# Row sums of 64 MiB: each partition takes 128 consecutive rows instead of eight groups of 16

## Chip, cores, metric

One core of one Trainium2 chip. The metric is the device time of one execution in microseconds (us).

## The reference

```python
batch, seq, dim = 32, 512, 1024
x = np.random.randn(batch, seq, dim).astype(np.float32)   # 67.1 MB
def reference(x):
    return np.sum(x, axis=-1).astype(np.float32)          # 16,384 sums
```

Every input byte is read once and added once; the output is 64 KB.

## The kernel before

The 16,384 rows are split over 128 partitions, 128 rows each. VectorE and ScalarE, two of the core's engines, sum rows out of on-chip tiles. The SP queue issues the loads, and 16 DMA engines carry them out in packets, here one packet for each contiguous run of a partition (896 of 64 KiB for the seven large loads). The rows are divided by groups: group g is a solid block of 2,048 rows (8 MiB), in which partition p has the 16 rows from 16p. Partitions that follow one another are therefore 64 KiB apart in device memory. The last group is split: its first 7 rows are the first load of the kernel, its last 9 rows the last four loads.

```python
    BIG, FIRST, pieces = 16, 7, (560, 464)
    x_g = x.flatten_outer_dims().rearrange("(g p j) d -> g p j d", p=P, j=BIG)
    out_v = out.rearrange("b s -> (b s)").rearrange("(g p j) -> p g j", p=P, j=BIG)
    def rows_from(j, n):
        return x_g[j // BIG, :, j % BIG : j % BIG + n, :]
    last = J // BIG - 1
    # ... three input buffers; rows() = one load and the sums of its rows
    t = inpool.tile([P, BIG * dim + 4], fp32)
    rows(t, 0, FIRST, last * BIG, 0)                    # 7 rows of the last group
    for g in range(last):                               # seven loads of 16 rows, 8 MiB each
        t = inpool.tile([P, BIG * dim + 4], fp32)
        if g < last - 1:
            load = rows(t, 0, BIG, g * BIG, 0)          # one VectorE reduce of 16 rows
        else:
            rows(t, 0, BIG, g * BIG, 7, pairs=True)     # 9 rows VectorE, 7 ScalarE
    # ... 6 rows, 2 rows, the last row in pieces of 560 and 464 elements
    hold(store(nc.scalar, 0, last), two, "its packets come behind those of the loads")
    # ... the last sums
    store(nc.sync, last, last + 1)
```

## Time and profile before

| | before |
|---|---|
| time, median of 3 runs | 161.56 us |
| span of the profiled execution | 160.0 us |
| first load landed | 11.10 us |
| last load landed | 157.90 us |
| load queue, share of the 16 DMA engines | 97.7% |
| VectorE busy | 120.6 us (75%) |
| one 16-row reduce, and the distance between two | 17.22 us, 19.36 us |

The DMA engines set the pace, since a tile takes 19.36 us to load and 17.22 us to sum. The lines that carry this are in the prediction.

### The profile page before, as it was taken

The page shows a single profiled execution, that of the slowest core. Times are in us where ns is not written, and L with a number is a line of the kernel's source. Part 1 is how long each engine was busy: PE and PEld are TensorE (multiplying, and loading weights), DVE is VectorE, ACT ScalarE, POOL GpSimd, SP SyncE. Part 2 cuts the span into 40 slices and gives each one's busy share as a digit, 9 for nine tenths or more (in the row PEclk, how much of TensorE's full clock was granted, in tenths as well). Part 3 has the DMA queues.
Part 4 walks back from the last instruction along what each step waited for, and adds up shares of the span by engine and source line. Part 5 has one row for each costly group of instructions (what it writes and reads, how often), then busy time and mean ns, then how long its engine had stood idle before and what let it go on. Part 6 is the DMA issues. An engine that isn't in the chain of part 4 may idle for free.

```text
span 160.0 us, 134 instructions
## 1 busy us (share of the span) xinstructions
DVE 120.6 (75%) x40; ACT 11.9 (7%) x21; POOL 0.2 (0%) x4
## 2 busy tenths in 40 slices
DVE  0029600399995999779995899949999499994955
ACT  3000000000000000000000000000000000003993
POOL 0000000000000000000000000000000000000000
DMA  8899899799699699699699798996996996996994
GB/s 322 365 491 524 377 410 524 328 459 524 278 508 524 262 524 524 262 524 524 262 524 442 344 524 377 410 524 262 524 524 262 524 524 262 524 524 264 424 384 123
DMA packets 2784, 67.18 MB, mean 420 GB/s; under 512 B 1248, under 2 KB 1376, under 8 KB 1504
## 3 DMA queue, kind: packets, MB, share of 16 engines
q1 hardware_dynamic: 1872, 67.12, 97.7%
q10 hardware_dynamic: 912, 0.06, 0.4%
HBM read 67.11 MB, written 0.07 MB: 420 GB/s over the span
## 4 chain that ended last, share of the span: by engine, by line
DMA 71%; DVE 27%; SPq 1%; issue 0%; DVEq 0%
DMA t<-in_x_dram 71%; DVE sums L167 26%; SPq L206 0%; SPq L248 0%; DVE t L181 0%; DVEq L279 0%
## 5 line engine op out<-in xcount | busy, mean ns | idle before, releaser
L167 DVE TENSOR_REDUCE sums<-t 128x16 f32<-128x16384 f32 (+1 forms) x7 | 110.9, 15848 | 33.7 <-DMA t<-in_x_dram 33.7
L194 ACT ACTIVATE unread<-t 128x1024 f32<-128x1024 f32 x10 | 10.1, 1013 | 145.1 <-DMA t<-in_x_dram 145.1
L181 DVE CUSTOM_DVE_ANT_0 t<-t 128x512 f32<-128x512 f32 (+2 forms) x16 | 9.6, 657 | 4.0 <-DMA t<-in_x_dram 3.8
L194 ACT ACTIVATION_READ_ACCUMULATOR unread<-t 128x1 f32 x10 | 1.9, 187 | 0.0
L194 ACT ACT_TABLE_LOAD x1 | 1.3, 1283 | 0.8 <-PEq L268 0.8
L181 DVE DVE_READ_ACCUMULATOR2_ANT sums<- 128x1 f32 x15 | 1.3, 84 | 0.0
L268 POOL MEMSET const-bfloat16-1.0<- 128x1 bf16 x1 | 0.1, 101 | 0.0
L268 POOL MEMSET const-uint8-127<- 128x1 uint8 x1 | 0.1, 101 | 0.0
L268 POOL MEMSET const-float32-0.0<- 128x1 f32 x1 | 0.1, 98 | 0.2 <-issue 0.2
L268 POOL MEMSET const-float32-1.0<- 128x1 f32 x1 | 0.1, 98 | 0.0
L181 DVE DVE_READ_ACCUMULATOR2_ANT t<- 128x1 f32 x1 | 0.1, 83 | 0.0
L246 DVE MEMSET t<- 128x1 f32 x1 | 0.1, 59 | 0.0
## 6 DMA issues: line engine op xcount, KB each, us to landing
t<-in_x_dram SPq DMA_DIRECT2D x1, 3584.0 KB, 11.1
t<-in_x_dram SPq DMA_DIRECT2D x1, 3072.0 KB, 28.8
t<-in_x_dram SPq DMA_DIRECT2D x1, 1024.0 KB, 30.9
t<-in_x_dram SPq DMA_DIRECT2D x1, 280.0 KB, 31.2
t<-in_x_dram SPq DMA_DIRECT2D x1, 232.0 KB, 31.2
t<-in_x_dram SPq DMA_DIRECT2D x7, 40.9
out_dram<-sums ACTq DMA_DIRECT2D x1, 56.0 KB, 2.1
out_dram<-sums SPq DMA_DIRECT2D x1, 8.0 KB, 1.4
```

What stands on the lines that cost most here:

```text
L167: return nc.vector.tensor_reduce(out=dst, in_=src, axis=mybir.AxisListType.X, op=mybir.AluOpType.add)
L181: return nc.vector.tensor_tensor_reduce(out=src[:, :n], in0=src[:, :n], in1=src[:, n:], scale=1.0, scalar=0.0, op0=mybir.AluOpType.add, op ...
L194: nc.scalar.activation(out=unread[:, :n], in_=src, func=mybir.ActivationFunctionType.Copy, accum_out=dst,)
L246: nc.vector.memset(whole[:, width + 1 :], 0.0)
L268: nc = _bacc.Bacc("TRN2", target_bir_lowering=False, num_devices=1)
```

## The change

Each partition now owns 128 consecutive rows. The stated arrangement of loads (7 rows, seven times 16, then 6, 2 and the last row in two pieces) stays. The code becomes simpler, the early store is one run of 448 bytes per partition instead of seven of 64, and in every load the partitions lie 512 KiB apart instead of 64 KiB. This distance is called the pitch below. Lines left out of the cut also make each tile 16 bytes shorter and put the last nine rows at the start of their tile.

```diff
-    x_g = x.flatten_outer_dims().rearrange("(g p j) d -> g p j d", p=P, j=BIG)
-    out_v = out.rearrange("b s -> (b s)").rearrange("(g p j) -> p g j", p=P, j=BIG)
-    def rows_from(j, n):
-        return x_g[j // BIG, :, j % BIG : j % BIG + n, :]
+    x_p = x.flatten_outer_dims().rearrange("(p j) d -> p j d", p=P)
+    out_p = out.rearrange("b s -> (b s)").rearrange("(p j) -> p j", p=P)
 ...
-            load = nc.sync.dma_start(out=block, in_=rows_from(j, n))
+            load = nc.sync.dma_start(out=block, in_=x_p[:, j : j + n, :])
 ...
-        rows(t, 0, FIRST, j, 0)
+        rows(t, 0, FIRST, 0, 0)
 ...
-                load = rows(t, 0, BIG, g * BIG, 0)
+                load = rows(t, 0, BIG, FIRST + g * BIG, 0)
 ...
-        hold(store(nc.scalar, 0, last), two, "its packets come behind those of the loads")
+        done = J - BIG
+        stored = nc.scalar.dma_start(out=out_p[:, :done], in_=sums[:, :done])
+        hold(stored, two, "its packets come behind those of the loads")
 ...
-        store(nc.sync, last, last + 1)
+        nc.sync.dma_start(out=out_p[:, done:], in_=sums[:, done:])
```

More of the change, by code (lines that the diff above doesn't have):

```diff
@@ L143 @@
     BIG = 16
-    x_g = x.flatten_outer_dims().rearrange("(g p j) d -> g p j d", p=P, j=BIG)
-    out_v = out.rearrange("b s -> (b s)").rearrange("(g p j) -> p g j", p=P, j=BIG)
-    def rows_from(j, n):
-        return x_g[j // BIG, :, j % BIG : j % BIG + n, :]
-    last = J // BIG - 1
+    x_p = x.flatten_outer_dims().rearrange("(p j) d -> p j d", p=P)
+    out_p = out.rearrange("b s -> (b s)").rearrange("(p j) -> p j", p=P)
     FIRST = 7
+    full = J // BIG - 1
     pieces = (560, 464)
@@ L214, in rows @@
             return load
-        def store(eng, g0, g1):
-            return eng.dma_start(
-                out=out_v[:, g0:g1],
-                in_=sums[:, g0 * BIG : g1 * BIG].rearrange("p (g j) -> p g j", j=BIG),
-            )
-        j = last * BIG
-        t = inpool.tile([P, BIG * dim + 4], fp32)
-        rows(t, 0, FIRST, j, 0)
+        t = inpool.tile([P, BIG * dim], fp32)
+        rows(t, 0, FIRST, 0, 0)
         first = sums_of[-1]
-        for g in range(last):
-            t = inpool.tile([P, BIG * dim + 4], fp32)
-            if g < last - 1:
-                load = rows(t, 0, BIG, g * BIG, 0)
+        for g in range(full):
+            t = inpool.tile([P, BIG * dim], fp32)
+            if g < full - 1:
+                load = rows(t, 0, BIG, FIRST + g * BIG, 0)
@@ L231 @@
             else:
-                rows(t, 0, BIG, g * BIG, 7, pairs=True)
+                rows(t, 0, BIG, FIRST + g * BIG, 7, pairs=True)
             if g == 1:
                 hold(load, first, "no descriptors of later loads while the first ones start")
-        t = inpool.tile([P, BIG * dim + 4], fp32)
-        rows(t, FIRST, 6, j + FIRST, 2, pairs=True)
-        two = rows(t, FIRST + 6, 2, j + FIRST + 6, 1, pairs=True)
-        a = BIG - 1
-        j += a
+        t = inpool.tile([P, BIG * dim], fp32)
@@ L244 @@
+        rows(t, 0, 6, J - 9, 2, pairs=True)
+        two = rows(t, 6, 2, J - 3, 1, pairs=True)
         c, width = pieces
-        whole = t[:, a * dim + c : BIG * dim + 2]
+        part = t[:, 8 * dim : 8 * dim + c]
+        whole = t[:, 8 * dim + c : 9 * dim + 2]
         nc.vector.memset(whole[:, width + 1 :], 0.0)
-        part = t[:, a * dim : a * dim + c]
-        nc.sync.dma_start(out=part, in_=rows_from(j, 1)[:, 0, :c])
-        nc.sync.dma_start(out=whole[:, 1 : width + 1], in_=rows_from(j, 1)[:, 0, c:])
@@ L250 @@
-        hold(store(nc.scalar, 0, last), two, "its packets come behind those of the loads")
+        nc.sync.dma_start(out=part, in_=x_p[:, J - 1, :c])
+        nc.sync.dma_start(out=whole[:, 1 : width + 1], in_=x_p[:, J - 1, c:])
+        done = J - BIG
+        stored = nc.scalar.dma_start(out=out_p[:, :done], in_=sums[:, :done])
+        hold(stored, two, "its packets come behind those of the loads")
         halves(whole[:, :1], part)
-        halves(sums[:, j : j + 1], whole)
-        store(nc.sync, last, last + 1)
+        halves(sums[:, J - 1 : J], whole)
```

## The prediction

> **What bounds the kernel now.** The whole input, 67.1 MB, must come in once, so I read the page for DMA first: the share of the queues, then the fill of the slices.
>
> ```profile
> DMA  8899899799699699699699798996996996996994
> GB/s 322 365 491 524 377 410 524 328 459 524 278 508 524 262 524 524 262 524 524 262 524 442 344 524 377 410 524 262 524 524 262 524 524 262 524 524 264 424 384 123
> ...
> q1 hardware_dynamic: 1872, 67.12, 97.7%
> q10 hardware_dynamic: 912, 0.06, 0.4%
> HBM read 67.11 MB, written 0.07 MB: 420 GB/s over the span
> ```
>
> The load queue keeps the 16 engines busy 97.7% of the span. The swing from 262 to 524 is only counting: a packet's bytes are booked where it ends, and packets are as long as a slice or so. Longer windows smooth it.
>
> ```profile
> 12.00:31.00 19.00, 7.30 (x2) 0.00 (x0) 0.00 (x0) 1.00 1.02 442
> 31.00:50.00 19.00, 16.87 (x2) 0.00 (x0) 0.00 (x0) 1.00 1.02 442
> 50.00:69.00 19.00, 17.02 (x1) 0.00 (x0) 0.00 (x0) 1.00 1.02 442
> 69.00:88.00 19.00, 17.22 (x1) 0.00 (x0) 0.00 (x0) 1.00 0.99 424
> ```
>
> Columns: window, its length, VectorE, ScalarE and GpSimd busy, clock, DMA share, GB/s. In each window the engines are full and VectorE is not. The timeline says the same by its idle times.
>
> ```profile
> 49.80 17.22 DVE L167 TENSOR_REDUCE sums<-t 128x16 f32<-128x16384 f32 x1 [2.13 <-DMA t<-in_x_dram]
> 69.16 17.22 DVE L167 TENSOR_REDUCE sums<-t 128x16 f32<-128x16384 f32 x1 [2.14 <-DMA t<-in_x_dram]
> 88.65 17.22 DVE L167 TENSOR_REDUCE sums<-t 128x16 f32<-128x16384 f32 x1 [2.27 <-DMA t<-in_x_dram]
> ```
>
> One 16-row tile is 128 x 64 KiB = 8.389 MB. Tiles become ready 19.36 us apart (69.16 - 49.80), a rate of 8.389 MB / 19.36 us = 433 GB/s, and VectorE needs 17.22 us of each interval; it waits 2.13 to 2.27 us every time. So the path is: first load, 56 packets of 64 KiB per DMA engine, the last small loads, the tail. The packet records in the trace make it sharper: 896 packets of 65,536 bytes with a median of 2,418 ns, and three quarters of them under 2,421 ns. 65,536 / 2,418 = 27.1 GB/s per engine, 433.7 GB/s for 16. So even a spread says that they run at one fixed rate[...].
>
> The chain of waits must be read with this in mind:
>
> ```profile
> 67.05 40.99 DMA t<-in_x_dram
> 108.04 0.02 issue
> 108.07 17.23 DVE sums L167
> ...
> 126.68 31.22 DMA t<-in_x_dram
> 157.90 0.06 issue
> 157.96 0.40 DVE t L181
> ```
>
> It puts 26.3% on VectorE, because a load is issued when a reduce frees its buffer (108.07 to 125.30). That is the order of issue, not a bottleneck: the loads issued at 125 us wait behind two others already queued, and land about 31 us later. The last load lands at 157.90, and 2.1 us of tail follow to the end of the span at 160.0. The measured time is 161.56, so 1.5 us lie outside the span.
>
> [...]
>
> [...]
>
> **The change part by part.**
>
> 1. Order of instructions: nothing moves. On VectorE one reduce of 7 rows, six of 16 rows, the same 14 halves of 512, memset and two last pieces; on ScalarE the same ten activations and one store; on the SP queue the same 12 loads with the same bytes per partition and one store. VectorE's 120.6 us and ScalarE's 11.9 us stay: 0. The three buffers rotate over the same nine tiles with the same waits: 0. The tile is 16 bytes shorter: no instruction sees it, 0.
>
> 2. Addresses of the loads. Before, in one load partition p starts at p x 64 KiB, so the 8 MB are one solid block. After, partition p starts at p x 512 KiB (128 rows x 4 KiB), and the block per partition stays 64 KiB solid. Packets keep their size and count: 896 of 64 KiB, 128 each of 28, 24 and 8 KiB, and the two pieces. Only the pitch changes, 64 KiB to 512 KiB, a power of two in both. What it costs is the one real unknown. Worth: bytes / rate = 67.11 MB / 433.7 GB/s = 154.7 us stand on the path, so each 1% of rate is 1.55 us, and it is not hidden: VectorE has 2.1 us per tile of slack in the wrong direction, it only waits longer. [...]here there are only reads[...]. I expect no loss or a small one to be likelier than the whole[...].
>
> 3. The early store (112 of 128 sums per partition). Before, seven runs of 64 B per partition, 896 packets; after, one run of 448 B, 128 packets. Its packets are short: 56 per engine at 8 to 11 ns plus 1 completion, about 0.6 us of engine time, saved to about 0.1 or 0.2. But when does it run? It is issued at 156.69 and lands 2.1 us later; in the records its packets start about 0.2 us after the last load packet has ended, and its last one ends about 0.9 us before the final store's first. It touches neither. So it comes off the busy time of the queue and not off the end: 0, at most -0.1.
>
> 4. Which sums the early store waits for. The new rows 0 to 111 end inside the last 16-row tile, at its nine VectorE rows; ScalarE's seven rows go with the final store. The store was held back by the 2-row load anyway and sits behind ScalarE's activations in its own queue. 0.
>
> 5. The final store. Before: 128 runs of 64 B that form a solid 8 KB; after: 128 runs of 64 B, 512 B apart. Issue to landing was 1.4 us, nearly all of it latency. I expect 1.3 to 1.6: 0.0, plus or minus 0.1 on the path.
>
> Sum: 161.56 + 0 + 1.0 + 0 + 0 + 0 = about 162.5.
>
> **Rivals.**
>
> A. The pitch costs nothing. For: the packets run at a fixed 27.1 GB/s per engine[...], the 64 KiB pitch was itself a large power of two[...]. Then the time is 161.3 to 161.8. This is the likeliest single outcome, about 55%.
>
> B. [...] For: [...]the 16 engines start within 0.8 us of each other. Already before, some tiles show stragglers: in the fourth large load packets of up to 2,528 ns, where the mean went to 2,443 (1% over the median)[...]. [...]
>
> C. The store pays off. For: 768 fewer packets, whole runs of 448 B. Against: step 3, neither lies on the path. At most 161.3. Even with a tail wholly free of store cost, only 2.1 us (1.3%) stand after the last load, so 2% cannot come from there[...]. Faster by 2% needs 158.3 us, which would be 154.7 us of data plus 1.4 us before the first packet plus the 1.5 outside with nearly no tail. I rule it out but for accident.
>
> D. VectorE becomes the bound. Against: its work is the same, 17.22 of 19.36 us per tile, and if loads slow down it gets further from it.
>
> **Range and chances.** Faster cases are bounded by A and C near 161.2. [...] With some 55% at A, 13% in between and 30% over 164.8 (2% over), I give 162.5 us, 161.2 to 167.5.
>
> **What would show it.** If A holds: tiles ready 19.3 to 19.5 us apart, waits of 2.1 to 2.3 us before each 16-row reduce, the 64 KiB packets at a median of 2,418 ns, the last load landing at 157.9. If B: [...]packet times longer and more spread, [...]the whole delay growing in proportion over the seven large loads, not in the tail. Steps 3 to 5: the ACT queue's packets fall from 912 to 144, its landing from 2.1 us to less, while the time from the last load to the end stays about 2.1 us. A change of more than 0.3 us in the tail, a change in VectorE's 17.22 us, or a load issued later relative to its reduce would prove the working wrong; so would a time under 161.

Passages of the prediction that no trace or run of this case shows are cut, at the marks. Its sum came to 162.5 us: the 161.56 us of the kernel before and 1.0 us for step 2. That 1.0 us stands as a bare estimate. Cut too are the sizes and some of the grounds of rival B, which holds that the loads' rate falls with the pitch, and with them what the upper end of the range and the 30% above 164.8 us rested on.

## The result

| | before | after |
|---|---|---|
| median of 6 runs | 161.78 us | 161.94 us |
| lowest to highest | 161.44 to 162.12 | 161.87 to 162.33 |

The ratio is 1.0016, with a 95% interval of 0.9999 to 1.0033. (A ratio is the mean time of one kernel's fast runs over that of the other's of the same rounds, so it is not quite the ratio of the medians.) The change is not clear of noise. The predicted 162.5 us was 0.6% above the 161.56 us that the prediction started from.

The page of the changed kernel, DMA queues:

```profile
q1 hardware_dynamic: 1872, 67.12, 97.4%
q10 hardware_dynamic: 144, 0.06, 0.1%
HBM read 67.11 MB, written 0.07 MB: 419 GB/s over the span
```

The load queue is as full as it was (97.4% against 97.7%). The ScalarE queue's packets fell from 912 to 144 as foreseen, and its store landed in 1.6 us instead of 2.1. The timeline of the changed kernel, with start, duration and, in brackets, the idle time before:

```profile
30.85 17.22 DVE L164 TENSOR_REDUCE sums<-t 128x16 f32<-128x16384 f32 x1 [11.71 <-DMA t<-in_x_dram]
50.20 17.22 DVE L164 TENSOR_REDUCE sums<-t 128x16 f32<-128x16384 f32 x1 [2.13 <-DMA t<-in_x_dram]
...
127.60 17.22 DVE L164 TENSOR_REDUCE sums<-t 128x16 f32<-128x16384 f32 x1 [2.12 <-DMA t<-in_x_dram]
```

Compare the idle times: 2.12 to 2.14 us in every interval, where a stream slower by 1% would have shown 2.3. The first and last of these starts are 96.75 us apart for five tiles, 19.35 us each. The kernel before, over the same five intervals:

```profile
30.45 17.22 DVE L167 TENSOR_REDUCE sums<-t 128x16 f32<-128x16384 f32 x1 [11.70 <-DMA t<-in_x_dram]
...
127.45 17.22 DVE L167 TENSOR_REDUCE sums<-t 128x16 f32<-128x16384 f32 x1 [2.16 <-DMA t<-in_x_dram]
```

That is 97.00 us, so in this pair of profiles the changed kernel's stream is the quicker one, by 0.25 us. The packet records agree: the 896 packets of 64 KiB have a median of 2,418 ns in both, and a mean of 2,426.5 ns before and 2,420.3 ns after. What went the other way is the start. The chain of waits of the changed kernel:

```profile
0.00 11.50 DMA t<-in_x_dram
...
126.85 31.18 DMA t<-in_x_dram
158.03 0.04 issue
158.07 0.40 DVE t L178
```

The first load lands at 11.50 us (before: 11.10), the last at 158.03 (before: 157.90). So in these two profiles 0.40 us are lost at the start and 0.27 come back in the stream. Two questions follow: is the lost start real, and does the stream, at 2,418 ns per packet with both pitches, escape because it is made of loads or because its runs are long?

### The profile page after: what moved, and what is told of

It is laid out like the page before. It is cut to its first block, busy times and chain, and to the rows that moved or that the text cites. A ratio compares the mean times of both kernels' runs of the same rounds, so it can differ in the third digit from the quotient of the medians.

```text
span 160.1 us, 134 instructions
## 1 busy us (share of the span) xinstructions
DVE 120.6 (75%) x40; ACT 11.9 (7%) x21; POOL 0.2 (0%) x4
## 3 DMA queue, kind: packets, MB, share of 16 engines
q1 hardware_dynamic: 1872, 67.12, 97.4%
## 4 chain that ended last, share of the span: by engine, by line
DMA 71%; DVE 27%; SPq 1%; issue 0%; DVEq 0%
DMA t<-in_x_dram 71%; DVE sums L164 26%; SPq L203 0%; SPq L235 0%; DVE t L178 0%; DVEq L268 0%
```

## The experiments

Kernels called wrong on purpose read or write permuted rows, so that one address pattern can be changed alone; their instructions, bytes and waits are those of the kernel that they start from.

### Which part of the change: loads and stores crossed

`a1_after_again` is the changed kernel again. `a2_newloads_oldstores` gives it the output addresses of before, `a3_oldloads_newstores` the reverse.

```diff
 a2, in the changed kernel
-    out=out_p[:, :done], in_=sums[:, :done]                # the final store likewise
+    out=out_g[:, :7], in_=sums[:, :done].rearrange("p (g j) -> p g j", j=BIG)
 a3, in the kernel before
-    out=out_v[:, g0:g1], in_=sums[:, g0 * BIG : g1 * BIG].rearrange(...)
+    out=out_p[:, g0 * BIG : g1 * BIG], in_=sums[:, g0 * BIG : g1 * BIG]
```

> The changed kernel once more, with five rounds. Theory 1 (the pitch costs the steady stream nothing[...]): 64 KiB packets at a median of 2,418 to 2,420 ns, ratio to before 1.000 to 1.003. Theory 2 (a small cost of the pitch at the start of a stream, seen as the first load landing at 11.5 instead of 11.1 us): the first load lands at 11.4 us or later in this profile again and the ratio is 1.001 to 1.003. Theory 3 (the 0.16% is spread of the runs): the first landing is anywhere between 11.0 and 11.6 us and the interval holds 1.

> Loads of the changed kernel (pitch 512 KiB), stores with the addresses of the kernel before (runs of 64 B, so the sums land in wrong places: the result is wrong on purpose). If the stores are off the path: same time as the changed kernel within 0.2 us, 912 packets on the ScalarE queue, its store landing after 2.1 us. If the shorter early store had gained something that the pitch took away: 0.3 us or more above the changed kernel, ratio to before 1.003 to 1.005.

> Loads of the kernel before (pitch 64 KiB), stores with the addresses of the changed kernel (448 B runs and 64 B at 512 B; the result is wrong on purpose). If the stores are off the path: ratio to before 0.999 to 1.001, the early store lands after 1.6 us, the final one after 1.4 us. If the new stores gain on the path: ratio 0.998 or less. If the first landing of 11.1 belongs to the 64 KiB pitch, it is below 11.3 us here; if it is chance, it may be anything from 11.0 to 11.6.

| five rounds, same chip | loads | stores | median us | ratio to before, 95% | first load landed |
|---|---|---|---|---|---|
| before | 64 KiB | 64 B runs | 161.51 | | |
| a1 | 512 KiB | 448 B runs | 162.01 | 1.0022 (1.0002 to 1.0041) | 11.52 |
| a2 | 512 KiB | 64 B runs | 161.87 | 1.0021 (1.0001 to 1.0041) | 11.33 |
| a3 | 64 KiB | 448 B runs | 161.47 | 0.9990 (0.9974 to 1.0006) | 10.98 |

With the new loads the ratio is 1.002 whichever the stores, and the interval just excludes 1; with the old loads it is 1 within the interval. So the stores are off the path within this noise, and the first landing goes with the loads. One line of a1's timeline shows that the steady stream repeats what the first profile of the change showed:

```profile
108.27 17.22 DVE L164 TENSOR_REDUCE sums<-t 128x16 f32<-128x16384 f32 x1 [2.13 <-DMA t<-in_x_dram]
```

### The disputed cost by itself: copies and loads at four pitches

The prediction argued for a cost of the pitch from copies within the device memory; no run had shown it. So copies are measured here beside loads. Four kernels first copy all rows into scratch memory (32 copies of 128 x 16 KiB), copy that a second time into another scratch array, and then run the changed kernel on the second copy. Source and target of the second copy have the same pitch: a solid block (b1), 512 KiB, 516 KiB or 2 MiB. The cut is of the last three; b1 copies 512 rows at a time as solid blocks, and its final loads have a pitch of 512 KiB.

```diff
+        far = far_t.rearrange("(p j) d -> p j d", p=P)      # far_t: [P * rows, dim] in device memory,
+        far2 = far2_t.rearrange("(p j) d -> p j d", p=P)    # rows = 128, 129 or 512 per partition
+        for i in range(0, J, 4):
+            nc.sync.dma_start(out=far[:, i : i + 4, :], in_=x_p[:, i : i + 4, :])
+        for i in range(0, J, 4):
+            nc.sync.dma_start(out=far2[:, i : i + 4, :], in_=far[:, i : i + 4, :])
+        x_p = far2
```

> All rows are copied twice within the device memory (32 copies of 128 x 16 KiB, each a solid 2 MB block on both sides), then the loads of the changed kernel read the second copy at a pitch of 512 KiB. The pass of interest is the second copy, memory to memory, and the final loads. Theory 1[...]: the second copy takes 2 x 67.1 MB / 433 GB/s = 310 us if both directions share one limit, or 155 us if read and write of one packet overlap; the final loads have 64 KiB packets at 2,418 ns as from the input.

> The same, every pass at a pitch of 512 KiB on both sides. [...] Final loads: 2,418 ns per 64 KiB packet under theory 1; 2,500 ns if pure reads suffer from the pitch at all.

> The same with a pitch of 516 KiB (129 rows) in the scratch memory, no power of two. [...] Final loads at 2,418 ns per 64 KiB packet.

> The same with a pitch of 2 MiB in the scratch memory. [...] The final loads tell two theories apart. Theory 1a (loads [...]only lose beyond some pitch): they slow visibly here, 64 KiB packets at 2,600 ns or more. Theory 1b ([...]the loss belongs to copies, where the writes have the pitch too): 2,418 to 2,440 ns here as well.

All four gave correct results. Time in windows (window, length, VectorE, ScalarE and GpSimd busy, clock, DMA share, GB/s, each packet counted once): the first line is inside the first copy, the second inside the second, the third inside the final loads. First 516 KiB, no power of two:

```profile
5.00:200.00 195.00, 0.00 (x0) 0.00 (x0) 0.00 (x0) 1.00 1.00 317
220.00:410.00 190.00, 0.00 (x0) 0.00 (x0) 0.00 (x0) 1.00 1.00 321
455.00:550.00 95.00, 84.33 (x6) 0.00 (x0) 0.00 (x0) 1.00 1.00 433
```

Then 512 KiB:

```profile
5.00:200.00 195.00, 0.00 (x0) 0.00 (x0) 0.00 (x0) 1.00 1.00 313
220.00:410.00 190.00, 0.00 (x0) 0.00 (x0) 0.00 (x0) 1.00 1.00 310
```

Then 2 MiB:

```profile
5.00:320.00 315.00, 0.00 (x0) 0.00 (x0) 0.00 (x0) 1.00 0.99 201
345.00:740.00 395.00, 0.00 (x0) 0.00 (x0) 0.00 (x0) 1.00 0.96 159
795.00:890.00 95.00, 84.33 (x6) 0.00 (x0) 0.00 (x0) 1.00 0.99 431
```

This answers the main question. The second copy at 512 KiB runs at 310 GB/s against 321 at 516 KiB, 3.4% less. That may be chance: the first copy of b2, also at 512 KiB on both sides, ran at 313, and each kernel ran once. At 2 MiB the second copy falls to 159, half; a later run, e2, repeats the two copies of b4 at 186 and 142 GB/s. So the fall is large in both, but its size differs by a tenth between single runs. But the third lines are the loads of the kernel under study, and they run at 431 GB/s at 2 MiB as they do at 516 KiB (433): the 64 KiB packets of the final loads have a median of 2,418 ns in all four kernels. (In b2 one of the five tile intervals is 19.98 us and the others 19.35 to 19.42; it holds one packet of 2,822 ns. The cause is not known.) So the loss belongs to copies and not to loads in runs of 64 KiB. The first pass says more: its reads are the same in b2, b3 and b4 (the input at 512 KiB), and only the target's pitch differs; 313 and 317 GB/s become 201 at 2 MiB. The target's pitch alone costs over a third. In the second pass the source has the pitch of 2 MiB too, and 201 becomes 159, so a copy seems to suffer from its reads as well, though no run separates that from other differences between the passes. Theory 1b, that the loss belongs to copies, stands, and 1a, that loads would show the loss beyond some pitch, falls for pitches up to 2 MiB.

Parts of the expectations of b1 to b4 are cut, at the marks: limits, and sizes of the loss, that no run had shown. The 2,500 ns left in b2's is a guess that no run shows either: the packets took 2,418 ns. b1's 155 or 310 us for the second copy missed: it took some 205 us, and the second copy of b3 some 210 us (67.1 MB / 321 GB/s). The b1 copy ran at 331 GB/s, but in packets of 64 KiB instead of 16 KiB, so it is no clean control for the pitch.

One reading did not fit: in b4 some of the small loads at the edges were slow. The 2,240-byte packets took 340 ns on average, against 93 ns in the changed kernel, while the 1,856-byte packets behind them took 75 ns, against 80 there. That raised a rival, theory L: the stream is safe only because its runs are long.

### Long runs or reads as such: the stream in runs of 4 KiB

Each large load reads its 16 rows as 16 separate runs, from a solid block (d1), at 512 KiB (d2) and at 508 KiB (d3); `e2_rt_2m_4k` does it in the 2 MiB round trip. Their outputs are wrong, which doesn't matter for the times.

```diff
 d2 and e2
-            load = nc.sync.dma_start(out=block, in_=x_p[:, j : j + n, :])
+            load = nc.sync.dma_start(out=block, in_=x_p[:, (j - FIRST) // BIG :: 8, :])   # loads of 16 rows
 d1: x as "(g c p) d -> p g c d";  d3: partition p from row 127 p
```

> The changed kernel, but each of the seven large loads reads its 16 rows as 16 runs of 4 KiB, out of a solid 8 MB block in which neighbouring partitions lie 4 KiB apart (the result is wrong on purpose). The control for the next run: what the packet size alone costs. With 14,336 packets of 4 KiB and some 9 ns of overhead each beside the 2,418 ns per 64 KiB: 160 to 170 us.

> The same packets of 4 KiB, with the 512 KiB between neighbouring partitions of the changed kernel (the result is wrong on purpose). Theory L (the long runs hide the pitch[...]): visibly slower than the control, 5 us or more. Theory R (loads do not suffer from this pitch whatever the run): within 1% of the control.

> The same with 508 KiB between partitions (127 rows, no power of two; the result is wrong on purpose). Theory L: equal to the control. Theory R: equal to both. If it is as slow as the 512 KiB run, it is the spread of the addresses and not the power of two.

> The round trip at a pitch of 2 MiB once more, with the seven large final loads cut into runs of 4 KiB (the result is wrong on purpose). Theory L for large pitches (long runs hide what short ones would show): packets well over the 164 ns of the runs with 512 KiB, 180 ns or more. Theory R (reads do not suffer): 164 ns and reduces 20.5 us apart, as there.

| packets of 4 KiB | solid (d1) | 512 KiB (d2) | 508 KiB (d3) | 2 MiB (e2) |
|---|---|---|---|---|
| median, mean ns | 164, 164.0 | 164, 163.8 | 164, 163.8 | 162, 164.7 |
| packets over 180 ns, of 14,336 | 47 | 0 | 0 | 213 |
| between tiles, mean of five, us | 20.48 | 20.48 | 20.48 | 20.72 |
| time of the kernel, us | 170.22 | 169.90 | 170.04 | with two copies |

Timeline of the 512 KiB run:

```profile
32.05 17.22 DVE L164 TENSOR_REDUCE sums<-t 128x16 f32<-128x16384 f32 x1 [12.85 <-DMA t<-in_x_dram]
...
134.44 17.22 DVE L164 TENSOR_REDUCE sums<-t 128x16 f32<-128x16384 f32 x1 [3.26 <-DMA t<-in_x_dram]
```

And of the 2 MiB run:

```profile
867.85 17.22 DVE L174 TENSOR_REDUCE sums<-t 128x16 f32<-128x16384 f32 x1 [13.38 <-DMA t<-far_t]
...
909.44 17.22 DVE L174 TENSOR_REDUCE sums<-t 128x16 f32<-128x16384 f32 x1 [3.47 <-DMA t<-far_t]
929.99 17.22 DVE L174 TENSOR_REDUCE sums<-t 128x16 f32<-128x16384 f32 x1 [3.33 <-DMA t<-far_t]
...
971.46 17.22 DVE L174 TENSOR_REDUCE sums<-t 128x16 f32<-128x16384 f32 x1 [3.78 <-DMA t<-far_t]
```

At 512 KiB five tiles take 102.39 us (134.44 - 32.05), 20.48 each, as they do from the solid block and at 508 KiB. So at the pitch of this change theory L falls: the stream does not need its long runs. A packet of 4 KiB takes 160 ns of an engine's time (20.48 us for 128 packets), 9 ns more than its share of a 64 KiB packet (2,418 / 16 = 151 ns; d1's expectation had the 9 ns as an estimate); the records overlap, since 128 of the recorded 164 ns would make 20.99 us.

At 2 MiB five tiles take 103.61 us (971.46 - 867.85), 20.72 each, 1.2% more, with single intervals from 20.47 to 21.00. So a small loss at 2 MiB, with short runs, is not excluded by this one profile; it is far from the halving of the copies. At the edges a pitch of 2 MiB shows plainly: in e2 again the 2,240-byte packets were slow (331 ns on average) and the 1,856-byte ones were not (75 ns). Those of the changed kernel, at 512 KiB, took 93 ns against 91 before.

### The start: the first load alone

`c1_first512` is the kernel before with only its first load at 512 KiB; `c2_first508` and its repetition `f1_first508_again` at 508 KiB (127 rows), `f2_first28` at 28 KiB, `f3_first256` at 256 KiB. `c3_firstsolid` is the changed kernel with only its first load put back to 64 KiB. Their outputs are wrong, which doesn't matter for the times.

```diff
 c1, c2, f1, f2, f3, in the kernel before: r = 128, 127, 127, 7, 64
+    x_f = x.flatten_outer_dims()[: P * r, :].rearrange("(p j) d -> p j d", p=P)
-            load = nc.sync.dma_start(out=block, in_=rows_from(j, n))
+            load = nc.sync.dma_start(out=block, in_=x_f[:, :n, :] if n == FIRST else rows_from(j, n))
 c3, in the changed kernel
+    x_f = x.flatten_outer_dims()[-P * BIG :, :].rearrange("(p j) d -> p j d", p=P)
```

> The kernel before with one thing changed: the first load (7 rows) is read at a pitch of 512 KiB instead of 64 KiB, all others stay (the result is wrong on purpose). If the 0.2% of the change lies in the first load alone: it lands at 11.3 to 11.5 us instead of 11.0 to 11.1, ratio to before 1.001 to 1.003. If it is spread over the stream: 11.1 us and 1.000.

> The same with a first load at a pitch of 508 KiB (127 rows): as far spread over the input, but no power of two (the result is wrong on purpose). If the engines' first packets hinder one another because the pitch is a power of two: lands at 11.0 to 11.1, ratio 1.000. If it is the spread over 64 MB that costs: 11.3 to 11.5, ratio 1.001 to 1.003, as at 512 KiB.

> The changed kernel with its first load alone put back to a pitch of 64 KiB (the result is wrong on purpose). If the cost lies in the first load: lands at 11.0 to 11.1, ratio to before 0.999 to 1.001. If it is spread over the stream: 1.002 as in the changed kernel.

A correct kernel that uses this was tried too. `e1_split` takes the first load from the first 896 rows as a solid block and gives each partition 121 of the other rows (pitch 484 KiB), with one small store more.

```diff
+    x_f = x_r[: P * 7, :].rearrange("(p j) d -> p j d", p=P)
+    x_p = x_r[P * 7 :, :].rearrange("(p j) d -> p j d", p=P)
```

> A correct version with the gain of both sides: the first load reads the first 896 rows as a solid block (pitch 28 KiB), every later load reads the other 15,488 rows at a pitch of 484 KiB (121 rows per partition, no power of two), stores in long runs, plus one more small store of 28 B runs beside the early one. If the first load is all that matters: lands at 10.9 to 11.1 us, ratio to before 0.997 to 1.000, some 0.4 us under the changed kernel. If the extra store gets in the way of the final one: 1.001 or more.

> The kernel before with the first load at a pitch of 508 KiB, a second profile of it (the result is wrong on purpose). If 11.04 us there was no chance: the first load lands at 10.9 to 11.2 us again. If landings simply scatter: it may be 11.3 to 11.5.

> The kernel before with the first load at a pitch of 28 KiB, one solid block as in the correct split version, where it landed at 11.24 us (the result is wrong on purpose). If a power of two alone decides: 11.0 to 11.1, and the 11.24 was scatter. If 28 KiB has a cost of its own: 11.2 to 11.3.

> The kernel before with the first load at a pitch of 256 KiB (the result is wrong on purpose). If the cost comes with a large power of two and grows with it: the first load lands between 11.1 and 11.4 us. If only 512 KiB and above have it: 11.0 to 11.1.

| run | pitch of first load / of the others | first load landed, us | median us | ratio to before, 95% |
|---|---|---|---|---|
| c1 | 512 / 64 KiB | 11.44 | 162.02 | 1.0029 (1.0014 to 1.0045) |
| c2 | 508 / 64 KiB | 11.04 | 161.69 | 1.0003 (0.9990 to 1.0017) |
| f1 | 508 / 64 KiB | 11.19 | 161.68 | 1.0010 (0.9995 to 1.0025) |
| f2 | 28 / 64 KiB | 11.23 | 161.71 | 1.0012 (0.9997 to 1.0027) |
| f3 | 256 / 64 KiB | 11.09 | 161.88 | 1.0027 (1.0010 to 1.0045) |
| c3 | 64 / 512 KiB | 10.98 | 161.46 | 0.9989 (0.9977 to 1.0001) |
| e1 | 28 / 484 KiB | 11.24 | 161.76 | 0.9997 (0.9981 to 1.0013) |

The first line of the chain of waits of c1, c2 and c3, in this order:

```profile
0.00 11.44 DMA t<-in_x_dram
0.00 11.04 DMA t<-in_x_dram
0.00 10.98 DMA t<-in_x_dram
```

The first landing follows the pitch of the first load, whatever the pitch of the others. Over all profiles with whole-run loads behind it, the four at 512 KiB landed at 11.33 to 11.52 us (the change, a1, a2, c1; mean 11.45), the eight at any other pitch at 10.98 to 11.24 (mean 11.11), and the two groups do not overlap. (In d1, d2 and d3 the first load is at 512 KiB too, with short runs behind it, and landed at 11.55 to 11.73.) So 512 KiB costs the first load 0.34 us; 508 KiB (two profiles), as far spread, does not, and 256 KiB (one profile) does not. (The expectation of f2 reserved 11.2 to 11.3 us for a cost of 28 KiB itself, and 11.23 fell there; but 508 KiB alone scatters from 11.04 to 11.19, so this is not shown.) The late start goes through to the end: the last sum starts at 158.10 us in a1 and at 157.59 in c3, 0.51 us of the 0.54 between their first landings. In the packet records the last of the 16 engines begins its first packet 1.13 to 1.26 us after the first one at 512 KiB, and 0.45 to 1.09 us at the others. Its packets themselves take no longer at 512 KiB (1,137 to 1,153 ns on average, 1,120 to 1,168 at the others). The mechanism behind that was not tried.

The whole times are less clean. f3 lands early and still has 1.0027. c1's profile shows why such sums waver: it has the stream of before, and these lines of its timeline stand out.

```profile
89.16 17.22 DVE L168 TENSOR_REDUCE sums<-t 128x16 f32<-128x16384 f32 x1 [2.37 <-DMA t<-in_x_dram]
108.67 17.22 DVE L168 TENSOR_REDUCE sums<-t 128x16 f32<-128x16384 f32 x1 [2.28 <-DMA t<-in_x_dram]
```

Tiles 19.51 us apart instead of 19.35 mean packets above the usual 2,418 ns, called stragglers below. Of 896 such packets, 60 to 102 took over 2,440 ns in four of the seven profiles with a 64 KiB stream (before, a3, c1, f3), and 3 to 10 in the other three and in all five with a stream at 512 or 484 KiB. They are worth up to half a microsecond, as much as the change itself (an estimate from the mean of the kernel before: 56 packets per engine x (2,426.5 - 2,418) ns = 0.48 us). Whether the 64 KiB pitch brings them or chance does, these few profiles do not settle. The correct split version e1 equals the kernel before (0.9997) and is no clear gain.

## Why the prediction was wrong

The measured 161.94 us lies inside the stated range, but the working has one wrong term: 0.6% more was forecast, 0.16% measured, and not clear of noise.

- The bound, right. The load queue stays at 97.4%, the 64 KiB packets at 2,418 ns, the reduces at 17.22 us with idle time before each of them.
- Step 1, order of instructions, and step 4, the rows of the early store: right, 0. Twelve loads, the same reduces and the same tail.
- **Step 2, addresses of the loads: the term that failed.** It put 1.0 us into the sum, spread over the stream, an estimate that no run of this case carried. The stream lost nothing: idle times of 2.12 to 2.14 us, five tiles in 96.75 us, and the same 2,418 ns at 2 MiB. What was said of copies was carried over to loads. Copies do lose here too (310 against 321 GB/s), but loads hold 431 GB/s at a pitch where copies fall to 159. The two are not alike in their sums either: the copies here moved 321 GB/s each way, 642 in sum, the loads 433. The doubt was in the text ("here there are only reads"), and in hindsight it should have decided for 0. Averaging two outcomes gave a number that neither would have given.
- What step 2 did not look for: a cost at the start. The first load lands 0.34 us later at 512 KiB. The prediction noted that the 16 engines start within 0.8 us of each other, but asked only about the rate; at 512 KiB the last one started 1.26 us after the first. That the whole came out a little above the kernel before is no merit of the 1.0 us: what excess there is came, as far as the profiles show, from this start, and the kernel before had stragglers that hid part of it.
- Step 3, early store: right. 912 packets became 144, landing went from 2.1 to 1.6 us, and crossing the stores changed nothing (1.0022 and 1.0021).
- Step 5, final store: right, 1.4 us with the runs adjacent or 512 B apart. Of these the packets fill 0.20 us (159.24 to 159.44) before and 0.21 after; the rest is the latency that step 5 speaks of.
- Rival A, the likeliest at 55%, with 161.3 to 161.8 us, is what the stream did. The 161.94 lies 0.14 us above it, less than the 0.34 us of the start. Rival B is excluded for loads at 512 KiB (tiles 19.35 us apart), and for runs of 64 KiB up to 2 MiB (431 GB/s). C gained nothing and D did not occur.
- "Stragglers" (102 of 896 packets over 2,440 ns before) were counted for rival B. They were all but absent (3 to 10) in all five profiles with a pitch of 484 or 512 KiB, so they were no evidence for B.

- Small slips that change nothing: the GB/s line of the page books a packet where it starts and not where it ends (the first slice of the kernel before has 322 GB/s on the page; its packet records give 323 by their starts and 208 by their ends); and the first packet starts at 0.99 us, not 1.4 as rival C has it.

Still open: the mechanism of the late start, the cause of the stragglers, whether short runs lose 1.2% at 2 MiB, and how the 0.16% divides, since both effects are of its size.

## What to carry to other kernels

Before using a bandwidth figure, check that it was measured for the same direction of transfer: here a pitch of 2 MiB, which cut a memory-to-memory copy in half (159 against 321 GB/s at 516 KiB), left a load in runs of 64 KiB at its rate (431 against 433). Where a stream of packets runs at one time per packet, as here at 2,418 ns, look for the effect of an address change at its edges too: here it showed at the first load (landed at 11.45 us on average at 512 KiB, 11.11 at other pitches), and at 2 MiB at a small last one (2,240-byte packets of 331 and 340 ns, against 93 at 512 KiB). And if two mechanisms give two distinct outcomes, predict the likelier and let the range cover the other; their mean is neither.
